# Pooling rows, gate additions and head 0's transposes around the seam between the gate stage and branch 1

## The chip, the cores and the metric

The kernel runs on one core of one Trainium2 chip. The metric is device time in microseconds (us) of one execution; three executions of the kernel before gave 874.96, 876.73 and 877.03 us, median 876.73 us. Lower is better.

## The reference

One encoder layer on 512 tokens of width 1024, all in float32:

```
proj = rms_norm(x) @ w_in           -> u_pool, u_lru, q, k, v, gate logits (3 x 1024)
gates = sigmoid(logits + b_gate)
pool:  for each of 4 groups of 256 channels (windows 2, 4, 8, 16):
         mean over the last w tokens, minus the token; then @ w_pool[g]; * pool_scale
lru:   width-4 convolution, two block-diagonal gates, a scan over the tokens
attn:  8 heads of 128, normalised q and k, strictly causal stick-breaking weights
merged = sum over branches of gates[b] * (y[b] @ w_branch[b])
x = x + merged @ w_out;  x = x + SwiGLU feed-forward(rms_norm(x))
```

## The kernel before

Every float32 product is taken as three matmuls of split operands (high times high, high times low, low times high). So nearly every operand is first split: ScalarE writes the high half (`act(..., AF.Copy)`), VectorE subtracts it from the source and writes the low half. For weights this is `split_w` (lines 142 and 143: `whi`, `wlo`); for pooled rows `split_hl` (L1040, L1041: `p00h`, `p00l` for group 0, half 0); for the pooling weights L1076 and L1077 (`wph`, `wpl`). Channels lie on the partitions, the 512 tokens along the free axis.

The kernel is written with a tile framework. The program lists the work; a planner at build time orders the instructions of each engine by their place in the program (a smaller place goes first, `tc.high_priority(n)` moves an instruction n places ahead) and by when a cost model says that they are ready, and assigns buffers. On the chip, each engine then runs its list in that fixed order and waits at semaphores. Two tools tie the order by hand: `tc.issue_after(ins)` puts what is traced inside it behind `ins` on `ins`'s engine, and `tc.add_manual_dep(a, b.name, ...)` does it for one pair. Neither adds a wait on the chip between engines.

The stages that matter here, in program order:

- **Pooling input** (249 to 287.7 us): 14 products `ps_ux`, `ps_uy` give u_pool in two chunks cc of 512 channels, each as two tiles j. The row (cc, j, n) is 128 channels; the group is 2 * cc + n. `pool_mean` (lines 945 to 961) makes a row's sliding-window mean on VectorE: for windows above 2 a short scan (L956), a long scan (L957), a short correction (L959) and the subtraction of the token (L961), with `pw` as the tile between. There are eight rows. Three run in this stage, the others in the next one.
- **Third branch's gates** (287.7 to 325.4 us): two chunks cc, each seven products `ps_gx`, `ps_gy` of 24 matmuls (L360). After product S4 of a chunk `gate_done` adds the bank `ps_gx` to the tile `gx` on VectorE (L939), after product 22 it does so for `ps_gy` and `gy`; ScalarE then takes two sigmoids (L941), and the POOL queue stores the tile (L943). In chunk 1, `pool_mean` is called after each of the products 12, S2, S1, S3 and S4 as long as rows are left; the last four rows, those of groups 2 and 3, run here. `load_early` fetches the weights of branch 1's first three half chunks, which are split here too.
- **Attention and the first two branches** (325.4 to some 474 us): `branch(1, c)`, c = 0 to 3, multiplies the scan's output `yHH`, `yHL` by `w_branch[1]`; a chunk is two half chunks of 24 matmuls (`half_chunk`; k-tiles 0 to 3, then 4 to 7; within a half, 12 matmuls for output tile j = 0 and 12 for j = 1), bank `ps_br` (L351 to L353); `merge` (L451) multiplies the result by its gate and frees the bank. `branch(0, c)` does the same with the pooled rows. Between them `tick()` pops attention tasks: a head's q and k are transposed (`trans`, L1131, tiles `pq`), split (L1134 `qkh`, L1135 `qkl`), multiplied into scores `z`, ScalarE takes sigmoids `K` and `A` (L1164, L1165), VectorE scans (`E`, L1168) and multiplies (`A`, L1170), the weights are transposed back (`pw`, L1181) and split (L1183, `wtl` L1184), and `py` is the head's output. `trans` of head 0 is first in program order in this stage. The pooled rows are split and multiplied by `w_pool` in `pool_split` and `pool_back` (banks `pps`, results `yph`, `ypl`), for all four groups ahead of branch 1 in program order.

[...] As the planner placed it, the last `ps_gx` lay on banks 0 and 1 and the last `ps_gy` on banks 4 and 5. In the next stage, head 0's `pq` of q is on bank 5, that of k on bank 7, the first `ps_br` on bank 0, the second on bank 2, and the third bank of that pool is 1. So head 0's first transposes can begin only when `gate_done` has read the last `ps_gy`, and branch 1's first matmuls when it has read the last `ps_gx`.

The scan's output comes back from DRAM in eight loads of 512 KB on the POOL queue (L1286: `yHH`, `yHL`); the last four of them, k-tiles 4 to 7, overwrite memory that the gate products read until S4 of chunk 1. SP's queue carries the other loads: `rawp` (w_pool, L1074), `raw` (branch weights, L150), `at` (q, k, v of a head, L1124), `g` (gates, L1101).

Of the kernel before, what the change touches and what calls it, by code (L numbers as in the profile page):

```python
# [12 lines left out]
ALU = mybir.AluOpType  # L13
# [3 lines left out]
P = 128  # L17
S = 512
D = 1024
KT = D // P  # L20
# [45 lines left out]
def layer_kernel(ctx: ExitStack, tc: tile.TileContext, x, xt, vecs, w_in, w_qkv7, w_gate7, w_pool7, w_pool, w_rg, w_ig,  # L66
# [282 lines left out]
    def mm3(ps, lh, ll, rh, rl, start, stop, skip=False, b=H):  # L349
        rh, rl = il(rh, b), il(rl, b)  # L350
        nc.tensor.matmul(ps, lh, rh, start=start, stop=False, skip_group_check=skip)  # L351
        nc.tensor.matmul(ps, lh, rl, start=False, stop=False, skip_group_check=skip)  # L352
        nc.tensor.matmul(ps, ll, rh, start=False, stop=stop, skip_group_check=skip)  # L353

# [54 lines left out]
    def half_chunk(pss, key, half, rhs, nticks, lo_last=False):  # L409
        wh, wl = weights(*key, half)  # L410
        if lo_last:

            for lo in range(2):
                for j in range(2):
                    for k in range(4 * half, 4 * half + 4):
                        for w, r in (((wl, 0),) if lo else ((wh, 0), (wh, 1))):
                            nc.tensor.matmul(pss[j], w[:, k % 4, j * P:(j + 1) * P], il(rhs[k][r]),
                                             start=k == 0 and not lo and r == 0,
                                             stop=k == KT - 1 and bool(lo))
            return  # L420
        for j in range(2):
            for kk in range(4):
                k = 4 * half + kk
                cs = slice(j * P, (j + 1) * P)
                mm3(pss[j], wh[:, kk, cs], wl[:, kk, cs], rhs[k][0], rhs[k][1],
                    k == 0, k == KT - 1)
            tick(nticks[j] if type(nticks) is tuple else nticks)
# [56 lines left out]
    with ExitStack() as first:  # L484
# [452 lines left out]
        def gate_done(cc, j, t, ps):  # L937
            v = two2(t)
            dve.tensor_tensor(v, v, in_order2(ps), ALU.add)  # L939
            for w in range(2):  # L940
# [4 lines left out]
        def pool_mean(cc, j, n):  # L945
# [43 lines left out]
        for cc in range(2):  # L989
# [11 lines left out]
            for nm in ORDER:  # L1001
# [42 lines left out]
    with ExitStack() as mix:  # L1044
# [27 lines left out]
        def load_pool_weights(g):  # L1072
            raw = rawp[g]
            state["rawp"] = nc.sync.dma_start(raw, w_pool[g].rearrange("(k p) c -> p k c", p=P)).ins  # L1074
            hi, lo = slot_r(f"wph{g}", (2, 256)), slot_r(f"wpl{g}", (2, 256))
            act(hi, raw, AF.Copy)  # L1076
# [34 lines left out]

        ysb = {}

        def head_tasks(h):
# [12 lines left out]
            def trans():  # L1127
                for t, gcol in ((0, qg), (1, vcol("k_norm"))):
                    pt = paux.tile([P, S], F32, tag="aux", name=f"pq{h}{t}")
                    for s in range(NS):  # L1130
                        nc.tensor.transpose(pt[:, s * P:(s + 1) * P], st["raw", t][:, s, :], idn)  # L1131
                    a = slot_r(f"qkh{h}{t}")
# [134 lines left out]
        tick(4)  # L1267
        for h in range(2):
            for g in (2 * h, 2 * h + 1):
                load_pool_weights(g)  # L1270
            if h:
                head0()
            for g in (2 * h, 2 * h + 1):
                for j in range(2):
                    pool_split(g, j)
        for g in range(4):
            for j in range(2):
                pool_back(g, j)
            tick()

# [10 lines left out]
        for c in range(4):  # L1291
            branch(1, c, ylru)
        hstack.close()

# [536 lines left out]
```

## Time and profile before

| | |
|---|---|
| median of 3 executions | 876.73 us (874.96 to 877.03) |
| profiled execution: its time, its span | 874.58 us, 872.8 us |
| granted TensorE clock, mean | 0.998 |
| TensorE (PE) busy | 859.7 us, 98% of the span |
| VectorE (DVE) busy | 748.5 us, 86% |
| ScalarE (ACT) busy | 528.3 us, 61% |
| GpSimd (POOL) busy | 96.6 us, 11% |
| DMA | 156.73 MB, mean 180 GB/s |

In the lists of instructions the columns are start in us, duration in us, engine, line, operation, output and inputs, and how often; a bracket at the end gives the idle time of the engine just ahead of it and what ended it ("issue": nothing that the profile shows). Where two operations of VectorE follow each other closely, the second starts a little ahead of the first's listed end, so steps are best taken from start to start. PEld is the weight load of a matmul, which overlaps with PE. "Granted clock" (PEclk) is the share of the full clock that TensorE had. A DMA's duration in these lists is that of its issue; when it lands is given apart.

### The profile page before, as it was taken

The page shows a single profiled execution, that of the slowest core. Times are in us where ns is not written, and L with a number is a line of the kernel's source. Part 1 is how long each engine was busy: PE and PEld are TensorE (multiplying, and loading weights), DVE is VectorE, ACT ScalarE, POOL GpSimd, SP SyncE. Part 2 cuts the span into 40 slices and gives each one's busy share as a digit, 9 for nine tenths or more (in the row PEclk, how much of TensorE's full clock was granted, in tenths as well). Part 3 has the DMA queues.
Part 4 walks back from the last instruction along what each step waited for, and adds up shares of the span by engine and source line. Part 5 has one row for each costly group of instructions (what it writes and reads, how often), then busy time and mean ns, then how long its engine had stood idle before and what let it go on. Part 6 is the DMA issues. An engine that isn't in the chain of part 4 may idle for free.

```text
span 872.8 us, 14573 instructions
## 1 busy us (share of the span) xinstructions
PE 859.7 (98%) x5707; PEld 791.0 (91%) x5707; DVE 748.5 (86%) x949; ACT 528.3 (61%) x733; POOL 96.6 (11%) x137
## 2 busy tenths in 40 slices
PE   9999999999999999999999999999999999999998
PEld 7888878888899997888889998889999999999998
DVE  6899897998786996997988696699998888899974
ACT  6554989657864466675664554455555555755642
POOL 1110002232325121000001200000000000031200
PEclk9999999999999999999999999999999999999999
DMA  9686356899598489545636865346543343798913
GB/s 340 165 294 191 97 168 193 239 296 260 194 269 232 93 240 303 184 129 153 210 97 168 177 186 193 97 121 169 140 127 98 104 115 107 230 247 201 195 36 122
DMA packets 114325, 156.73 MB, mean 180 GB/s; under 512 B 8272, under 2 KB 86096, under 8 KB 114256
## 3 DMA queue, kind: packets, MB, share of 16 engines
q1 hardware_dynamic: 100864, 107.30, 38.4%
q0 software_dynamic: 13248, 48.24, 23.9%
q8 instruction: 45, 0.74, 0.3%
q10 hardware_dynamic: 144, 0.26, 0.1%
q14 instruction: 24, 0.20, 0.1%
HBM read 135.33 MB, written 18.87 MB: 177 GB/s over the span
## 4 chain that ended last, share of the span: by engine, by line
PE 87%; DVE 5%; ACT 4%; issue 2%; DMA 1%; SPq 0%; DVEq 0%; ACTq 0%
PE ps_y L360 11%; PE ps_q L876 8%; PE ps_x L360 8%; PE ps_dy L1749 6%; PE ps_dx L1749 5%; PE ps_br L351 3%; PE ps_br L352 3%; PE ps_br L353 3%; PE ps_bY L1373 2%; PE ps_gy L360 2%; PE ps_gate L779 2%; PE ps_gx L360 2%; PE ps_uy L360 2%; PE ps_bX L1373 2%; PE ps_lru L351 1%
## 5 line engine op out<-in xcount | busy, mean ns | idle before, releaser
L142 ACT ACTIVATE whi<-raw 128x1024 fp32r<-128x1024 f32 x58 | 61.1, 1054 | 56.3 <-PE ps_out L352 15.1
L143 DVE TENSOR_TENSOR wlo<-raw,whi 128x1024 fp32r<-128x1024 f32 x58 | 70.9, 1223 | 12.3 <-ACT whi L142 11.4
L142 ACT ACTIVATE whi<-qw 128x1024 fp32r<-128x1024 f32 x48 | 50.4, 1054 | 30.2 <-PE ps_q L876 11.9
L143 DVE TENSOR_TENSOR wlo<-qw,whi 128x1024 fp32r<-128x1024 f32 x48 | 58.3, 1221 | 10.3 <-ACT whi L142 10.3
L1534 ACT ACTIVATE wh_S<-w_S 128x1024 fp32r<-128x1024 f32 x36 | 38.3, 1063 | 28.7 <-PE ps_y L360 20.0
L1655 POOL DMA_DIRECT2D dw<-in_w_down_dram x20 | 17.3, 882 | 303.7 <-DMA dw<-in_w_down_dram 260.6
L1535 DVE TENSOR_TENSOR wl_S<-w_S,wh_S 128x1024 fp32r<-128x1024 f32 x36 | 44.0, 1224 | 3.3 <-ACT wh_S L1534 3.3
L1534 ACT ACTIVATE wh<-w 128x1024 fp32r<-128x1024 f32 x27 | 28.7, 1064 | 27.7 <-PE ps_x L360 9.4
L1535 DVE TENSOR_TENSOR wl<-w,wh 128x1024 fp32r<-128x1024 f32 x27 | 33.1, 1225 | 7.9 <-ACT wh L1534 7.9
L1534 ACT ACTIVATE whdS<-dw 128x1024 fp32r<-128x1024 f32 x20 | 21.3, 1063 | 21.0 <-PE ps_dy L1749 10.6
L1168 DVE TENSOR_TENSOR_SCAN E<-K,ahead 128x512 f32<-128x512 f32 (+3 forms) x32 | 25.4, 816 | 8.7 <-ACT K L1164 8.7
L1535 DVE TENSOR_TENSOR wldS<-dw,whdS 128x1024 fp32r<-128x1024 f32 x20 | 24.3, 1223 | 5.5 <-ACT whdS L1534 5.5
L351 PE MATMUL ps_br<-yHH,whi 128*128 128x512 f32 x64 | 24.9, 390 | 0.1
L352 PE MATMUL ps_br<-yHL,whi 128*128 128x512 f32 x64 | 24.6, 384 | 0.0
L351 PE MATMUL ps_lru<-HH,whi 128*128 128x512 f32 x64 | 24.6, 384 | 0.0
L351 PE MATMUL ps_br<-yph,whi 128*128 128x512 f32 x64 | 24.5, 383 | 0.0
L353 PE MATMUL ps_br<-yHH,wlo 128*128 128x512 f32 x64 | 24.4, 384 | 0.0
L143 DVE TENSOR_TENSOR wlo<-pw,whi 128x1024 fp32r<-128x1024 f32 x13 | 15.8, 1223 | 10.0 <-ACT whi L142 8.6
L351 PE MATMUL ps_gate<-HH,whi 128*128 128x512 f32 x64 | 24.4, 381 | 0.0
L352 PE MATMUL ps_lru<-HL,whi 128*128 128x512 f32 x64 | 24.3, 379 | 0.0
L353 PE MATMUL ps_lru<-HH,wlo 128*128 128x512 f32 x64 | 24.3, 379 | 0.0
L352 PE MATMUL ps_gate<-HL,whi 128*128 128x512 f32 x64 | 24.3, 379 | 0.0
(786 smaller groups left out, 3552.2 us busy)
## 6 DMA issues: line engine op xcount, KB each, us to landing
qw<-in_w_qkv_dram SPq DMA_DIRECT2D x24, 512.0 KB, 7.0
raw<-in_w_in_dram SPq DMA_DIRECT2D x23, 512.0 KB, 5.6
dw<-in_w_down_dram POOLq DMA_DIRECT2D x20, 512.0 KB, 7.8
w<-in_w_ffn_gate_dram SPq DMA_DIRECT2D x36, 256.0 KB, 4.0
w<-in_w_ffn_up_dram SPq DMA_DIRECT2D x36, 256.0 KB, 4.6
raw<-in_w_branch_dram SPq DMA_DIRECT2D x13, 512.0 KB, 3.9
qw<-in_w_qkv_dram POOLq DMA_DIRECT2D x12, 512.0 KB, 7.7
qd<-r POOLq DMA_DIRECT2D x12, 512.0 KB, 6.8
```

Source lines behind the costliest of these rows:

```text
L142: act(hi, raw, AF.Copy)
L143: los.append(dve.tensor_tensor(lo, raw, hi.bitcast(F32), ALU.subtract).ins)
L351: nc.tensor.matmul(ps, lh, rh, start=start, stop=False, skip_group_check=skip)
L352: nc.tensor.matmul(ps, lh, rl, start=False, stop=False, skip_group_check=skip)
L353: nc.tensor.matmul(ps, ll, rh, start=False, stop=stop, skip_group_check=skip)
L360: nc.tensor.matmul(o, a_[a][:, w, k, :], il2(b_[b][:, k, :]), start=first and n == k == 0, stop=last and n == 2 and k == 3, skip_group_che ...
L876: nc.tensor.matmul(ps[:, a, :], b_[:, k, ts_], il(a_[:, kk, :]), start=first and n == k == 0, stop=n == 2 and k == 3, skip_group_check=True)
L1168: dve.tensor_tensor_scan(E[:, c0:c0 + n][:, ::-1], K[:, c0 + 1:c0 + n + 1][:, ::-1], ahead[:, S - n:][:, ::-1], 0.0, ALU.mult, ALU.add)
L1373: nc.tensor.matmul(o, ah[x_][:, w, k, :], il2(b[k][y_]), start=first_ and n == k == 0, stop=n == 2 and k == 3, skip_group_check=True)
L1534: act(h, src, AF.Copy)
L1535: dve.tensor_tensor(l, src, h.bitcast(F32), ALU.subtract)
L1749: nc.tensor.matmul(o, a_[a][:, w, k0 + k, :], il2(b_[b][:, k, :]), start=first and i == k == 0, stop=last and i == 2 and k == nk - 1, skip ...
```

## The change

Four edits go together.

1. In the gate stage `gate_done`'s addition gets 60 places of priority, and the one that comes last (chunk 1, j = 1, the `gy` tile) is remembered in `state["last"]`. The gate stage calls `pool_mean` once, after product S2 of chunk 0, and no more in chunk 1; the four rows that are left, all of them of groups 2 and 3, are called after the stage's last product and are tied behind `state["last"]` on VectorE.
2. `load_pool_weights` is cut in two: the loads of all four groups are called together, and `split_pool_weights` is called with each group.
3. Groups 0 and 1 are split and multiplied as before ahead of branch 1, with two ticks after each where there was one after each of four groups. Groups 2 and 3 are split and multiplied after `branch(1, 0)`, tied behind the last weight split that has been traced by then.
4. The eight transposes of head 0 are tied behind the last of the 24 matmuls of branch 1's first half chunk on TensorE.

The three matmuls in `mm3`, the number of pooling rows, splits, transposes and products, and what they compute, stay as they were.

```diff
@@ half_chunk
-                mm3(pss[j], ..., k == 0, k == KT - 1)
+                last = mm3(pss[j], ..., k == 0, k == KT - 1)
+            state.setdefault((key, half, j), last)
             tick(nticks[j] if type(nticks) is tuple else nticks)
@@ gate_done
-            dve.tensor_tensor(v, v, in_order2(ps), ALU.add)
+            with tc.high_priority(60):
+                last = dve.tensor_tensor(v, v, in_order2(ps), ALU.add).ins
+            if cc and j:
+                state["last"] = last
@@ pool_mean
-            with tc.issue_after(los[-1]):
+            with tc.issue_after(state["last"] if "last" in state else los[-1]):
@@ the gate stage's loop
-                if (cc or nm == "S2") and nm not in ("11", "22") and means:
+                if (cc, nm) == (0, "S2"):
                     pool_mean(*means.pop(0))
+        for row in means:
+            pool_mean(*row)
@@ the attention stage
-        for h in range(2):
-            for g in (2 * h, 2 * h + 1):
-                load_pool_weights(g)
-            if h:
-                head0()
-            for g in (2 * h, 2 * h + 1):
+        for g in range(4):
+            load_pool_weights(g)
+        head0()
+
+        def pool_group(g, edge):
+            with edge:
+                split_pool_weights(g)
                 for j in range(2):
                     pool_split(g, j)
-        for g in range(4):
+
+        for g in range(2):
+            pool_group(g, nullcontext())
+        for g in range(2):
             for j in range(2):
                 pool_back(g, j)
-            tick()
+            tick(2)
...
         for c in range(4):
             branch(1, c, ylru)
+            if c == 0:
+                for g in range(2, 4):
+                    pool_group(g, tc.issue_after(los[-1]))
+                    for j in range(2):
+                        pool_back(g, j)
+            if c == 0:
+                for tr in first_trans:
+                    tc.add_manual_dep(tr, state[("br", 1, 0), 0, 1].name, ...NoSync...)
```

More of the change, by code (lines that the diff above doesn't have):

```diff
@@ L352, in mm3 @@
         nc.tensor.matmul(ps, lh, rl, start=False, stop=False, skip_group_check=skip)
[L353 removed]
+        return nc.tensor.matmul(ps, ll, rh, start=False, stop=stop, skip_group_check=skip).ins
     def product(a_, b_, ps, half, first, last, ws=(0, 1)):
@@ L1074, in load_pool_weights, with split_pool_weights @@
             state["rawp"] = nc.sync.dma_start(raw, w_pool[g].rearrange("(k p) c -> p k c", p=P)).ins
+        def split_pool_weights(g):
+            raw = rawp[g]
             hi, lo = slot_r(f"wph{g}", (2, 256)), slot_r(f"wpl{g}", (2, 256))
@@ L1130, in trans @@
                     for s in range(NS):
-                        nc.tensor.transpose(pt[:, s * P:(s + 1) * P], st["raw", t][:, s, :], idn)
+                        tr = nc.tensor.transpose(pt[:, s * P:(s + 1) * P], st["raw", t][:, s, :], idn).ins
+                        if h == 0:
+                            first_trans.append(tr)
                     a = slot_r(f"qkh{h}{t}")
```

7 lines of the change are left out of this document (5 added, 2 removed).

## The prediction

> **What bounds the kernel now.** I read the page's busy shares, then the waits of TensorE, then the instructions around the longest one, then busy time by stretch.
>
> ```profile
> PE 859.7 (98%) x5707; PEld 791.0 (91%) x5707; DVE 748.5 (86%) x949; ACT 528.3 (61%) x733; POOL 96.6 (11%) x137
> ```
>
> TensorE is busy for 859.7 of 872.8 us, and the change takes no matmul away. All that it can win lies in the 13.1 us of idle time and in matmuls that run slowly. The waits of TensorE (us in total, times, longest) show one large one:
>
> ```profile
> PE pq L1131 <- issue: 3.7, 1, 3.7
> ```
>
> It is head 0's transposes, at the seam that the change edits. Here are TensorE's instructions there, and, from a warm stretch, the same eight transposes and three matmuls again:
>
> ```profile
> 325.12 0.28 PE L360 MATMUL ps_gy<-hT4h,wlo 128*128 128x256 f32 x1
> 329.11 1.94 PE L1131 MATMUL pq<-idn,at 128*128 128x128 f32 x8 [3.72 <-issue]
> 331.99 0.38 PE L351 MATMUL ps_br<-yHH,whi 128*128 128x512 f32 x1
> 332.21 0.38 PE L352 MATMUL ps_br<-yHL,whi 128*128 128x512 f32 x1
> ...
> 418.05 1.04 PE L1131 MATMUL pq<-idn,at 128*128 128x128 f32 x8
> 419.58 0.38 PE L351 MATMUL ps_br<-yph,whi 128*128 128x512 f32 x1
> ```
>
> What does it wait for? VectorE's list answers:
>
> ```profile
> 312.29 0.17 DVE L956 TENSOR_TENSOR_SCAN pw<-u,zero 128x8 f32<-128x8 f32 x1
> 314.46 1.22 DVE L143 TENSOR_TENSOR wlo<-qw,whi 128x1024 fp32r<-128x1024 f32 x1
> ...
> 322.22 0.18 DVE L956 TENSOR_TENSOR_SCAN pw<-u,zero 128x16 f32<-128x16 f32 x1
> 324.40 1.22 DVE L143 TENSOR_TENSOR wlo<-rawbr,whi 128x1024 fp32r<-128x1024 f32 x1
> 325.53 1.22 DVE L939 TENSOR_TENSOR gx<-gx,ps_gx 128x1024 f32<-128x1024 f32 x1
> 326.66 1.22 DVE L143 TENSOR_TENSOR wlo<-rawbr,whi 128x1024 fp32r<-128x1024 f32 x1
> 327.80 1.22 DVE L939 TENSOR_TENSOR gy<-gy,ps_gy 128x1024 f32<-128x1024 f32 x1
> 329.15 1.23 DVE L143 TENSOR_TENSOR wlo<-rawbr,whi 128x1024 fp32r<-128x1024 f32 x1
> 331.05 0.75 DVE L1135 SCALAR_TENSOR_TENSOR qkl<-pq,qg,qkh 128x512 fp32r<-128x512 f32 x1 [0.67 <-ACT qkh L1134]
> 340.92 1.22 DVE L1168 TENSOR_TENSOR_SCAN E<-K,ahead 128x512 f32<-128x512 f32 x1 [7.76 <-ACT K L1164]
> ```
>
> The `gy` addition ends at 329.02, and the transposes, whose bank it frees, start at 329.11. It is late because VectorE spent 312.29 to 324.40 on four pooling rows between weight splits. The `gx` addition began only at 325.53, though its product was over by 322.9, when a load that waits for the same product went out; and the split of branch 1's first weights ran at 324.40, though its high half had been begun at 319.95:
>
> ```profile
> 319.95 1.06 ACT L142 ACTIVATE whi<-rawbr 128x1024 fp32r<-128x1024 f32 x1 [1.13 <-PE ps_gy L360]
> 322.90 0.53 POOL L1286 DMA_DIRECT2D yHL<-ydl  x1 [10.30 <-PE ps_gx L360]
> ```
>
> The table by stretch (busy us of PE, PEld, DVE, ACT, POOL with their counts, then granted clock, DMA share, GB/s) shows what follows:
>
> ```profile
> 325.40:329.10 3.70, 0.00 (x0) 0.02 (x1) 3.61 (x4) 2.26 (x3) 0.54 (x1) 0.91 0.90 258
> 329.10:332.00 2.90, 2.89 (x12) 2.68 (x13) 2.17 (x3) 2.83 (x6) 1.26 (x4) 0.53 1.06 359
> 332.00:340.90 8.90, 8.90 (x45) 7.91 (x44) 1.16 (x2) 1.06 (x3) 1.32 (x4) 1.00 0.98 333
> 340.90:385.40 44.50, 43.12 (x225) 34.97 (x224) 42.08 (x64) 34.79 (x66) 0.00 (x0) 1.00 0.59 177
> 385.40:476.00 90.60, 90.04 (x508) 80.29 (x507) 80.22 (x141) 55.80 (x115) 3.51 (x4) 1.00 0.52 147
> ```
>
> Three things are to be seen. The stall leaves TensorE at 0.53 of its clock until 332. VectorE then has a hole, 332.0 to 340.9, with 1.16 us of work. And from 340.9 to 385.4 VectorE is busy for 42.08 of 44.5 us: there it is as much the limit as TensorE, and only after 385.4 does it have room again (80.22 of 90.6).
>
> **The change part by part.** *Stall.* With the rows out of the way, the `gx` addition runs at about 323 and ends before 325.4, so branch 1's first bank is free. Its first weights can be split at about 321. Branch 1's 24 matmuls then follow the last gate product directly, 24 x 0.215 = 5.2 us (step 331.99 to 332.21), to 330.6. The `gy` addition runs at 325.45 to 326.67 below them, so the transposes find their bank free. The 3.72 us go. If the cover fails (branch 1's operands late), the transposes would still start at 326.7, so 2.3 of the 3.72 stay won.
>
> *Clock.* From 329.11 to 331.99 eight transposes and three matmuls take 2.88 us; warm, from 418.05 to 419.58, the same take 1.53. The stall so costs another 1.35 us, and TensorE's gain is 3.72 + 1.35 = 5.07 us. [...]
>
> *Rows.* A row takes 2.17 us (312.29 to 314.46), and the last 2.18, so the four take 8.69 us. They are moved from a place where VectorE's time was, in part, free to right behind the `gy` addition. What VectorE gets: the addition ends 2.35 us earlier (326.67 for 329.02); the hole of 7.76 and the 0.67 us ahead of `qkl` can be filled. What it pays is 8.69. So VectorE as a whole gets ahead by 2.35 + 7.76 + 0.67 - 8.69 = 2.1 us, against TensorE's 5.1. The two weight splits and the `gx` addition of 324.40 to 327.80 move into the place that the rows leave.
>
> *What the difference does.* Low halves feed TensorE, and in 340.9 to 385.4 weight loads already wait for VectorE:
>
> ```profile
> PEld pq L1131 <- DVE wtl L1184: 1.1, 2, 0.8
> PEld z L352 <- DVE qkl L1135: 0.7, 2, 0.4
> ```
>
> A TensorE that comes 5.1 us early meets operands that come 2.1 us early, and waits more often. VectorE can win at most its idle 44.5 - 42.08 = 2.4 us more by 385.4, so the stage's gain has the bounds 2.1 and 4.5 us, and below 2.1 if the order leaves new holes on VectorE. I take 2.8, near the lower end: of these 2.4 us, 1.9 are three waits of `ypl` for `yph`
>
> ```profile
> DVE ypl L1095 <- ACT yph L1094: 1.9, 3, 0.7
> ```
>
> in the pooling groups, and I give a third of them, 0.7 us, to the groups' being spread out; nothing else in the change touches the rest.
>
> *Groups 2 and 3 later.* No work is added. Their rows are ready at about 337.6 (326.67 + 8.69, and two weight splits of 1.14 that go first). Before, their first split came 14 us after that:
>
> ```profile
> 351.81 0.69 DVE L1041 TENSOR_TENSOR p20l<-u,p20h 128x512 fp32r<-128x512 f32 x1
> ```
>
> So I cost this at nothing. The cover is branch 1's first chunk and groups 0 and 1; without it, groups 2 and 3 would wait for the rows, some 8.7 us at most.
>
> *Queues.* SP's loads of w_pool go into memory that no row of the four uses, and were out by 319.4, ahead of the seam; they cost nothing. But `raw` loads wait for the splits that free their buffer, and these come earlier. POOL's loads of the scan's output keep their place, behind the gate products:
>
> ```profile
> 300.28 19.11 SPq L1074 DMA_DIRECT2D rawp<-in_w_pool_dram  x4
> 324.45 0.57 POOL L1286 DMA_DIRECT2D yHL<-ydl  x1
> DMA to landing us min/median/max: 8.5/8.5/8.5
> 325.64 0.37 SPq L150 DMA_DIRECT2D raw<-in_w_branch_dram  x1
> 327.91 0.37 SPq L150 DMA_DIRECT2D raw<-in_w_branch_dram  x1
> ```
>
> (The line on landing is that of the `yHL` load of 324.45.) It lands at 333.0. The second half chunk starts at 330.6 + 0.8 (transposes) = 331.4 and reaches k-tile 6, which needs it, six matmuls later, at 332.7: a wait of 0.3 us, where before the half chunk came after the landing. TensorE is ahead of VectorE by then, so I add nothing.
>
> *Sum.* 5.1 us won on TensorE, 2.3 given back between 336 and 385 for VectorE's low halves: 2.8 us. The profiled execution took 874.58 us (span 872.8 and 1.8 around it) and would take 871.8. It was 2.15 us below the median of 876.73; on the median, I predict 873.9 us.
>
> **The rivals.** *TensorE keeps all of it.* If the planner fills the wait with branch matmuls (the third bank of `ps_br` takes 12 more, 2.6 us) and VectorE catches up in the roomier stretch after 385.4, all 5.1 us stay: 871.6 us. For it: TensorE waited little after 385.4 (90.04 of 90.6 busy). Against it: VectorE's 2.1.
>
> *A transfer takes the stall's place.* DMA is at 1.06 of its share from 329.1 to 332 and 0.98 to 340.9. Two `raw` loads of 512 KB come some 3 us earlier and share with the scan's output. Each is 1.4 us at 359 GB/s; if both go ahead, the last `yHL` lands at 335.8 and TensorE waits 3.1 us from 332.7. Of these 2.3 are what it would have waited for VectorE anyway, and 0.8 more are lost; where the later waits don't shrink for it, nearly all is. The time is 874.7 to 876.7, say 875.3.
>
> *Slower: the rows stand ahead of head 0 and the pooling splits.* VectorE runs its list in order, and the four rows are earlier in the program than `qkl` and `p00l`. The case has such a block already, on ScalarE:
>
> ```profile
> 283.76 0.69 DVE L961 SCALAR_TENSOR_TENSOR u<-pw,u 128x512 f32<-128x512 f32 x1
> 340.13 0.69 ACT L1164 ACTIVATE K<-z,qrs 128x512 f32<-128x512 f32 x1 [7.84 <-PE z L353]
> 341.81 0.63 ACT L1040 ACTIVATE p00h<-u 128x512 fp32r<-128x512 f32 x1
> ```
>
> Row 0 is ready at 284.4, yet its `p00h` stands behind `K`. With the rows first, until 337.6, two `qkl` (1.4 us) end at 339.0 and six splits of groups 0 and 1 (0.6 each) at 342.6. TensorE is through with branch 1's first chunk at 331.4 + 5.2 = 336.6. If its list has `pps` next, it waits until 342.6: 6.0 us, and 1.35 for the clock, which is 7.4 against 5.1 won: 2.3 us slower, 879.0 us. It decides from a wait of about 5 us; with `z` or 12 branch matmuls next the wait is 2.4 us or less, which is my forecast. [...]
>
> **How the numbers follow.** Chances: my forecast 0.48, all kept 0.20, transfer 0.15, slower 0.17. The forecast's own range is 872.2 (2.1 + 2.4 us) to 875.2 (1.5 us: the lower end with one new hole on VectorE of about the 0.67 us ahead of `qkl`). The whole range runs from 871.3, just past the full gain, to 878.0, halfway into the slower case. A measurement of this kernel tells about 0.3% from no change, 2.6 us, so faster begins below 874.1. All of the second case and two thirds of the first lie there: 0.52. The last third of the first and most of the transfer's give 0.29 within, and the slower case with a remainder 0.19.
>
> **What would show it.** Right: no wait of `pq` at 325; the first `ps_br` within 0.2 us of the last `ps_gy`; clock 1.00 from 325 to 332; the `gx` addition ending before 325.4; VectorE without the hole ahead of the first `E`, busy from 326.7 to about 342; more or longer waits of TensorE for `qkl`, `p..l` and `wtl` between 336 and 385, by some 2 us. Wrong: a wait of the first `ps_br` for the `gx` addition or a weight split; a wait for `yHL` beyond 1 us near 332; a single wait above 5 us at the first `pps` or `z`; or waits between 340 and 385 no larger than before, which would leave all 5.1 us.

## The result

The changed kernel took 872.3 us (median of 5 runs, 871.77 to 872.74) and the kernel before 876.73 us (median of 5 runs beside it, 873.88 to 877.28): a ratio of 0.9958, 95% interval 0.994 to 0.9976, so 2.1 to 5.3 us faster. Timed once more on another occasion it took 872.09 us against 874.32, a ratio of 0.9977 (0.9963 to 0.999). Both say faster; the first occasion's 4.4 us is not all the change's doing, as the stage lengths below show.

The profiled execution took 872.3 us with a span of 870.5 (before: 874.58 and 872.8).

### The profile page after: what moved, and what is told of

The parts are those of the page before. It is cut to its first block, busy times and chain, and to the rows that moved or that the text cites. A ratio compares the mean times of both kernels' runs of the same rounds, so it can differ in the third digit from the quotient of the medians.

```text
span 870.5 us, 14573 instructions
## 1 busy us (share of the span) xinstructions
PE 859.6 (99%) x5707; PEld 789.9 (91%) x5707; DVE 748.4 (86%) x949; ACT 528.2 (61%) x733; POOL 95.1 (11%) x137
## 4 chain that ended last, share of the span: by engine, by line
PE 86%; DVE 6%; ACT 5%; DMA 2%; issue 1%; SPq 0%; DVEq 0%; ACTq 0%
PE ps_y L360 11%; PE ps_q L877 8%; PE ps_x L360 8%; PE ps_dy L1774 6%; PE ps_dx L1774 5%; PE ps_uy L360 2%; PE ps_gate L780 2%; PE ps_bY L1398 2%; PE ps_gy L360 2%; PE ps_br L353 2%; PE ps_br L352 2%; PE ps_br L351 2%; PE ps_gx L360 2%; PE ps_bX L1398 2%; PE ps_ux L360 2%; PE ps_lru L351 1%
## 5 line engine op out<-in xcount | busy, mean ns | idle before, releaser
L1180 DVE TENSOR_TENSOR_SCAN E<-K,ahead 128x512 f32<-128x512 f32 (+3 forms) x32 | 25.4, 816 | 2.0 <-ACT K L1176 2.0
L353 PE MATMUL ps_gate<-HH,wlo 128*128 128x512 f32 x64 | 24.3, 379 | 0.0
```

The costliest lines, as they stand in the source:

```text
L353: return nc.tensor.matmul(ps, ll, rh, start=False, stop=stop, skip_group_check=skip).ins
L1180: dve.tensor_tensor_scan(E[:, c0:c0 + n][:, ::-1], K[:, c0 + 1:c0 + n + 1][:, ::-1], ahead[:, S - n:][:, ::-1], 0.0, ALU.mult, ALU.add)
```

## The profile after

The lines of code have moved: `gate_done`'s addition is L941, the pooling rows are L960 to L965, the transposes L1141, `qkl` L1147, `E` L1180, the loads of the scan's output L1302. The busy shares, from the page, are as good as the same; it is the span that is shorter.

```profile
PE 859.6 (99%) x5707; PEld 789.9 (91%) x5707; DVE 748.4 (86%) x949; ACT 528.2 (61%) x733; POOL 95.1 (11%) x137
```

TensorE's instructions at the seam, from the timeline:

```profile
325.18 0.28 PE L360 MATMUL ps_gy<-hT4h,wlo 128*128 128x256 f32 x1
325.30 0.38 PE L351 MATMUL ps_br<-yHH,whi 128*128 128x512 f32 x1
330.48 1.04 PE L1141 MATMUL pq<-idn,at 128*128 128x128 f32 x8
332.72 0.48 PE L351 MATMUL ps_br<-yHH,whi 128*128 128x512 f32 x1
334.26 0.48 PE L352 MATMUL ps_br<-yHL,whi 128*128 128x512 f32 x1 [1.05 <-DMA yHL<-ydl]
335.55 0.38 PE L353 MATMUL ps_br<-yHH,wlo 128*128 128x512 f32 x1
337.09 0.48 PE L352 MATMUL z<-qkl,qkh 128*128 128x512 f32 x1 [1.16 <-DVE qkl L1147]
```

The 3.72 us stall is gone: branch 1 follows the last gate product after 0.12 us, and the transposes take 1.04 us where they took 1.94. Two waits that weren't there stand behind them: 1.05 us for the last load of the scan's output, and 1.16 us for head 0's low half. The profile counts idle time from the modelled end of the matmul before; from start to start each wait is longer. From 332.72 to 334.26 it is 1.54 us, and from 335.55 to 337.09 as well, where such matmuls otherwise start 0.22 us apart; the matmul behind each starts 0.10 us late too (334.58 and 337.41). So TensorE loses 1.4 us at each. VectorE's timeline shows what that low half was behind:

```profile
322.82 1.22 DVE L941 TENSOR_TENSOR gx<-gx,ps_gx 128x1024 f32<-128x1024 f32 x1 [0.47 <-PE ps_gx L360]
...
325.50 1.22 DVE L941 TENSOR_TENSOR gy<-gy,ps_gy 128x1024 f32<-128x1024 f32 x1 [0.32 <-PE ps_gy L360]
326.63 1.22 DVE L143 TENSOR_TENSOR wlo<-rawbr,whi 128x1024 fp32r<-128x1024 f32 x1
327.77 0.33 DVE L960 TENSOR_TENSOR_SCAN pw<-u,zero 128x8 f32<-128x8 f32 x3
...
335.02 0.69 DVE L965 SCALAR_TENSOR_TENSOR u<-pw,u 128x512 f32<-128x512 f32 x1
335.63 0.74 DVE L1147 SCALAR_TENSOR_TENSOR qkl<-pq,qg,qkh 128x512 fp32r<-128x512 f32 x1
336.29 0.74 DVE L1147 SCALAR_TENSOR_TENSOR qkl<-pq,vt,qkh 128x512 fp32r<-128x512 f32 x1
...
338.68 1.23 DVE L1180 TENSOR_TENSOR_SCAN E<-K,ahead 128x512 f32<-128x512 f32 x1 [1.04 <-ACT K L1176]
```

The four rows run from 327.77 to 335.63 (7.86 us, their parts woven into one another), then `qkl`, on which `z` waits. Head 0's high halves had been written by 332.38 (`qkh` on ScalarE), so it is the rows that hold `qkl` back. The profile lists no idle time of VectorE from 325.50 to the end of the second `qkl` at 337.03, and `z` starts 0.06 us after that. The table by stretch (busy us of PE, PEld, DVE, ACT, POOL with their counts, then granted clock, DMA share, GB/s):

```profile
325.20:330.50 5.30, 5.30 (x28) 4.61 (x27) 5.00 (x9) 2.63 (x4) 2.60 (x7) 1.00 1.13 316
330.50:332.00 1.50, 1.50 (x12) 1.42 (x11) 1.50 (x3) 0.88 (x2) 0.74 (x2) 1.00 1.12 381
332.00:340.90 8.90, 6.37 (x29) 4.42 (x28) 7.82 (x14) 3.92 (x9) 0.00 (x0) 1.00 1.05 354
340.90:385.40 44.50, 43.34 (x232) 35.56 (x231) 41.92 (x64) 33.65 (x63) 0.00 (x0) 1.00 0.60 174
385.40:473.80 88.40, 87.83 (x494) 78.31 (x493) 78.26 (x138) 54.68 (x114) 3.51 (x4) 1.00 0.52 145
```

The clock stays at 1.00. TensorE's new idle time, 2.53 us, lies in the third stretch. In the fourth, where the prediction expected it, TensorE idles 44.50 - 43.34 = 1.16 us; before it was 44.50 - 43.12 = 1.38.

**A cleaner measure than the median.** The executions of the kernel before scatter over some 4 us, so I take the length of the stage that the change edits: from the start of the last `ps_gy` matmul to that of the first `ps_bY`, the first product after the attention stage. Its end rows in the kernel before and in the changed one:

```profile
474.26 0.27 PE L1373 MATMUL ps_bY<-B11h,whi 128*128 128x256 f32 x1
```

```profile
472.07 0.27 PE L1398 MATMUL ps_bY<-B11h,whi 128*128 128x256 f32 x1
```

With 325.12 and 325.18 as their starts: 149.14 us before, 146.89 after. Two other stretches of the same profiles, worked out in the same way, are not the change's: from the first `ps_u` to the last `ps_gy`, and from the first `ps_y` to the last matmul. The fourth column is the first part of the seam stage: from the start of the last `ps_gy` to that of the first `z` matmul that reads a `qkl`. In every kernel of the table 46 other matmuls lie between them (8 transposes, 36 of branch 1, 2 of `z`). All profiles of this study but one (the filled stall further down, which has ten matmuls more and another order behind):

| kernel | first `ps_u` to last `ps_gy` | **seam stage** | of it up to the first `z<-qkl` | first `ps_y` to last matmul |
|---|---|---|---|---|
| before | 76.14 | **149.14** | 14.32 | 273.01 |
| before, again | 74.93 | **149.16** | 14.34 | 276.83 |
| changed | 75.71 | **146.89** | 11.91 | 273.03 |
| changed, again | 75.57 | **146.96** | 11.99 | 273.79 |
| changed, timed again | 74.92 | **146.95** | 12.00 | 273.02 |
| without edit 4 | 74.92 | **146.96** | 12.00 | 274.84 |
| without edit 3 | 74.93 | **146.84** | 12.00 | 273.01 |
| without edit 1 | 76.15 | **145.68** | 10.83 | 273.02 |
| edit 4 alone | 74.92 | **145.58** | 10.76 | 275.32 |
| three rows back | 75.68 | **144.99** | 10.14 | 275.29 |
| three rows back, again | 74.93 | **145.01** | 10.14 | 273.01 |
| three rows back, small loads | 75.54 | **145.75** | 10.88 | 273.00 |

The seam stage of one kernel repeats within 0.07 us, in the three kernels that were profiled more than once; the outer columns move by 1.2 and by 3.8 us, also between two profiles of the same kernel. So the change won 2.25 us (149.14 to 146.89), and differences of 1 us between variants can be read from this column where the medians can't carry them. The fourth column says where they arise: what is left of the stage behind that `z` is 134.82 to 134.98 us in every kernel. So nearly all that these edits win or lose lies in the first 10 to 14 us.

## The experiments

The theory behind the first runs was the prediction's: the edits together take the stall away, and VectorE's lateness takes part of it back. Each of the first four undoes one part of the change.

**Without edit 4.** The changed kernel, with the transposes free to go where the planner puts them:

```diff
             if c == 0:
-                for tr in first_trans:
-                    tc.add_manual_dep(tr, state[("br", 1, 0), 0, 1].name, ...NoSync...)
```

> The change without its fourth edit: head 0's transposes are not tied behind branch 1's first 24 matmuls, and come first on TensorE again. The theory (a late addition held the transposes' bank; two waits then give part of it back) expects: the gy addition ends at about 326.7 as in the changed kernel, so the transposes wait some 1.3 us from 325.4, too short to cost much clock; the second half chunk comes 1.3 us later and so no longer waits for the load of the scan's output (1.05 us in the changed kernel). Together within 0.5 us of the changed kernel, 872 to 873 us. The rival (the tie is what removes the stall) expects a wait of 3 us or more for the transposes and 875 us or more.

871.67 us, ratio 0.9973 (0.9961 to 0.9984). TensorE's timeline:

```profile
325.65 1.06 PE L1141 MATMUL pq<-idn,at 128*128 128x128 f32 x8 [1.36 <-issue]
333.62 0.48 PE L352 MATMUL ps_br<-yHL,whi 128*128 128x512 f32 x1 [0.22 <-DMA yHL<-ydl]
336.01 0.48 PE L352 MATMUL z<-qkl,qkh 128*128 128x512 f32 x1 [0.71 <-DVE qkl L1147]
```

The transposes now wait 1.36 us, and the clock stays at 1.00 from 324 to 332. But the waits behind them shrink by as much (1.05 to 0.22, 1.16 to 0.71): those operands come when they come, and a TensorE that is 1.4 us later finds them nearer. The seam stage is 146.96 against 146.89: given the other edits, edit 4 is worth nothing. With or without it, `z` starts 11.9 to 12.0 us after the last `ps_gy`, when the second `qkl` is there.

**Without edit 1.** The rows back between the weight splits of the gate stage, no priority for the additions; edits 2 to 4 kept:

```diff
-            with tc.high_priority(60):
-                last = dve.tensor_tensor(v, v, in_order2(ps), ALU.add).ins
-            if cc and j:
-                state["last"] = last
+            dve.tensor_tensor(v, v, in_order2(ps), ALU.add)
...
-            with tc.issue_after(state["last"] if "last" in state else los[-1]):
+            with tc.issue_after(los[-1]):
...
-                if (cc, nm) == (0, "S2"):
+                if (cc or nm == "S2") and nm not in ("11", "22") and means:
                     pool_mean(*means.pop(0))
-        for row in means:
-            pool_mean(*row)
```

> The change without its first edit: the four pooling rows and the gate additions stand in the gate stage as before, everything else is as in the changed kernel, and TensorE's list is the same. The theory expects the first bank of branch 1 to wait for the gx addition until about 326.8, 1.4 us, and in return no wait of z for qkl (1.16 us in the changed kernel) and none for the load of the scan's output (1.05 us), as VectorE has 8.7 us less to do behind the seam: 870.5 to 872.5 us, no slower than the changed kernel. The rival (moving the rows is what wins) expects the stall of 3 us or more back at the first matmul of branch 1, and 875 us or more.

870.61 us, ratio 0.9959 (0.9946 to 0.9973); seam stage 145.68. TensorE, and then VectorE:

```profile
326.70 0.48 PE L351 MATMUL ps_br<-yHH,whi 128*128 128x512 f32 x1 [1.48 <-DVE gx L940]
```

```profile
325.43 1.21 DVE L940 TENSOR_TENSOR gx<-gx,ps_gx 128x1024 f32<-128x1024 f32 x1
333.34 0.75 DVE L1142 SCALAR_TENSOR_TENSOR qkl<-pq,qg,qkh 128x512 fp32r<-128x512 f32 x1 [3.06 <-ACT qkh L1141]
337.25 1.23 DVE L1175 TENSOR_TENSOR_SCAN E<-K,ahead 128x512 f32<-128x512 f32 x1 [1.91 <-ACT K L1171]
```

One wait of 1.48 us for the `gx` addition, and then neither `yHL` nor `qkl` is waited for beyond 0.3 us. VectorE has holes of 3.06 and 1.91 us again, and yet the stage is 1.2 us shorter than with edit 1. Edit 1 as a whole, in a kernel that has edit 4, costs 1.2 us net.

**Three rows back.** One row alone stays behind the `gy` addition; the priority stays:

```diff
-                if (cc, nm) == (0, "S2"):
+                if (cc, nm) == (0, "S2") or cc and nm in ("12", "S2", "S1"):
                     pool_mean(*means.pop(0))
```

> The changed kernel with three of its four moved rows back in the gate stage (after its products 12, S2 and S1) and only the last one behind the gy addition; TensorE's list is the same. The theory expects both gate additions on time (no wait at 325), the wait of z for qkl gone, the load's wait of 1.05 us still there, and fewer waits of TensorE for VectorE up to 385: 1.2 to 2.5 us below the changed kernel, 869.8 to 871.1 us. The rival (VectorE's list behind the seam is no limit, the waits at qkl only move TensorE's idle time) expects 872.0 to 872.6 us, as the changed kernel.

871.56 us, ratio 0.9963 (0.9948 to 0.9977); seam stage 144.99, the shortest. TensorE's timeline:

```profile
329.89 1.04 PE L1141 MATMUL pq<-idn,at 128*128 128x128 f32 x8
333.23 0.48 PE L352 MATMUL ps_br<-yHL,whi 128*128 128x512 f32 x1 [0.79 <-DMA yHL<-ydl]
```

No wait at the seam, none over 0.3 us for `qkl`, and 0.79 us for the load. Against the kernel without edit 1 the stage is 0.7 us shorter, with the additions on time; so the priority and one moved row together cost nothing, and what costs 1.9 us in the changed kernel is that three more rows stand ahead of `qkl`. The total missed what was expected: the last stage took 275.29 us in the profile, 2.3 more than in most others, in code that is the same. A later run settles that.

**Without edit 3.** All four pooling groups ahead of branch 1, as in the kernel before, the other edits kept:

```diff
-        for g in range(2):
+        for g in range(4):
             pool_group(g, nullcontext())
-        for g in range(2):
+        for g in range(4):
             for j in range(2):
                 pool_back(g, j)
-            tick(2)
+            tick()
...
-            if c == 0:
-                for g in range(2, 4):
-                    pool_group(g, tc.issue_after(los[-1]))
-                    for j in range(2):
-                        pool_back(g, j)
```

> The changed kernel with its third edit undone: pooling groups 2 and 3 are split and multiplied ahead of branch 1 in program order again, with one tick after each group. The theory gives the spreading 0.7 us of the forecast's 2.8 (a third of the 1.9 us of waits for yph): 872.7 to 873.5 us, with waits of ypl for yph of about 1.9 us. The rival (the cover is needed: groups 2 and 3 would wait for the late rows) expects a wait of TensorE for p20l or p30l above 2 us and 874.5 us or more.

871.48 us, ratio 0.9968 (0.9956 to 0.998); seam stage 146.84 against 146.89. VectorE's waits (us in total, times, longest) from 325 to 390, in this variant:

```profile
DVE ypl L1104 <- ACT yph L1103: 1.8, 3, 0.7
```

and in the changed kernel:

```profile
DVE vl L1154 <- ACT vh L1153: 1.3, 1, 1.3
DVE qkl L1147 <- ACT qkh L1146: 0.9, 1, 0.9
```

The spreading does take the three waits of `ypl` away, and about as much of other waits on VectorE takes their place. TensorE waits elsewhere than in the changed kernel:

```profile
330.85 0.46 PE L351 MATMUL ps_br<-yHH,whi 128*128 128x512 f32 x1 [0.68 <-DMA yHH<-ydh]
334.06 0.48 PE L352 MATMUL ps_br<-yHL,whi 128*128 128x512 f32 x1 [1.18 <-DMA yHL<-ydl]
```

It stands longer for the loads, 1.86 us in all, and then only 0.10 us for `qkl`. Yet `z` starts 12.00 us after the last `ps_gy`, as in the changed kernel. While four rows stand ahead of `qkl`, the waits for the loads are hidden in the one that ends with `qkl`. Behind `z` the stage takes 134.84 us in this variant and 134.98 in the changed kernel, so the spreading wins nothing there either.

**Edit 4 alone.** If edit 1 costs 1.2 us beside edit 4, and edit 3 nothing, then the tie alone in the kernel before should do as well as without edit 1 (the lines that remember the last matmul, as in the change, are left out here):

```diff
@@ the kernel before
                     for s in range(NS):
-                        nc.tensor.transpose(pt[:, s * P:(s + 1) * P], st["raw", t][:, s, :], idn)
+                        tr = nc.tensor.transpose(pt[:, s * P:(s + 1) * P], st["raw", t][:, s, :], idn).ins
+                        if h == 0:
+                            first_trans.append(tr)
...
             branch(1, c, ylru)
+            if c == 0:
+                for tr in first_trans:
+                    tc.add_manual_dep(tr, state[("br", 1, 0), 0, 1].name, ...NoSync...)
```

> The kernel before with edit 4 alone: head 0's eight transposes behind the first 24 matmuls of branch 1; the four pooling rows, the order of the groups and the loads stay as in the kernel before. Theory (edit 4 alone takes the stall away, and moving the rows costs a little over 1 us): the same matmul order as in the variant with the rows in their old place, so a wait of some 1.4 us for the addition of gx or gy stays in front of the first ps_br, no long wait for the transposed inputs at 325, none over 0.5 us for yHL or qkl; the stretch from the last ps_gy to the first ps_bY about 145.7 us, against 149.1 in the kernel before and 146.9 in the changed one; the total some 3 us under the kernel before. Rival (edit 4 needs edits 1 and 3: with the old order of the groups, VectorE and the transfers are late for the transposes wherever they stand): the stretch stays at 148 us or more, with a wait of 2 us or more at the transposes or at the first ps_br, and the total within 1 us of the kernel before.

871.78 us, ratio 0.9953 (0.9935 to 0.9972). TensorE's timeline:

```profile
323.67 0.28 PE L360 MATMUL ps_gy<-hT4h,wlo 128*128 128x256 f32 x1
325.35 0.48 PE L351 MATMUL ps_br<-yHH,whi 128*128 128x512 f32 x1 [1.40 <-DVE gx L940]
330.63 1.04 PE L1133 MATMUL pq<-idn,at 128*128 128x128 f32 x8
...
469.25 0.27 PE L1381 MATMUL ps_bY<-B11h,whi 128*128 128x256 f32 x1
```

145.58 us: 3.56 us under the kernel before, by one edit. The two ways to end the stall don't add up. Edit 4 alone wins 3.56; edits 1 to 3 without it win 2.18; all four win 2.25. The fourth column shows why: with edit 1 the four rows keep `z` from starting before 11.9 us, whatever TensorE waits for until then, and without edit 1 it starts at 10.8. The stage of this variant was profiled once, and the intervals of its ratio and of the changed kernel's overlap; the comparison rests on the stage.

**Three rows back, the last loads in halves.** What is left there is the wait for `yHL`. The four loads of 512 KB become eight of 256 KB, in the order of use, on top of the edit above:

```diff
-            for k2 in range(2):
+            step = 1 if i else 2
+            for k in range(0, 4, step):
                 for t, d in zip(yhl, yd):
-                    load = nc.gpsimd.dma_start(t[:, 2 * k2:2 * k2 + 2, :], d[i][:, 2 * k2:2 * k2 + 2, :]).ins
+                    load = nc.gpsimd.dma_start(t[:, k:k + step, :], d[i][:, k:k + step, :]).ins
```

> The variant with three rows back in the gate stage, and the last four loads of y (512 KB each) cut into eight of 256 KB in the order of use, so that the first slice that TensorE needs can land sooner. Theory (the wait for yHL is for the landing of these loads, whose bytes share the queue): the wait for yHL, 0.79 us in the variant with three rows back and 1.05 us in the changed kernel, falls under 0.3 us, and the stretch from the last ps_gy to the first ps_bY goes from 144.99 to 144.2 to 144.7 us; the total 869 to 871 us. Rival (the loads share the transfer engines and are all in flight together, so smaller ones land no sooner; four more issues on POOL also delay the stores of gx and gy by some 2 us): the wait for yHL stays at 0.6 to 1.2 us, the stretch at 145 us or more.

870.98 us, ratio 0.9941 (0.9921 to 0.9962). TensorE's timeline:

```profile
332.79 0.48 PE L352 MATMUL ps_br<-yHL,whi 128*128 128x512 f32 x1 [0.46 <-DMA yHL<-ydl]
333.71 0.48 PE L351 MATMUL ps_br<-yHH,whi 128*128 128x512 f32 x1 [0.22 <-DMA yHH<-ydh]
```

The one wait has become several: these two, 0.68 us together, and a short one of 0.13 us for `yHL` at 334.64. The first slice comes 0.14 us sooner (its wait ends 8.49 us after the last `ps_gy`, against 8.63 with large loads), and the next two come 0.9 and 1.9 us behind it. The first wait, 0.46 us, lies between what the theory and the rival expected; the seam stage, 145.75, is the rival's. It is 0.75 us longer than with large loads, and the fourth column has 0.74 of that (10.88 against 10.14): the waits for the loads, from start to start, are the whole difference. The median of 870.98 is no sign of the best variant, as the kernel before took 875.7 us beside it.

**The kernel before, again, and the changed kernel, again.** No edit; these are the measure of the measure.

> The kernel before, unchanged, for a second profile. Theory (the stretch from the last ps_gy to the first ps_bY is a property of the kernel, and the stages around it vary from run to run): the stretch 148.6 to 149.6 us again, the wait for the transposed inputs 3.4 to 4.0 us, and the clock lowered after it again. Rival (the lowered clock came by chance): the wait is the same and the clock stays at 1.00, and the stretch is some 1.3 us shorter, about 147.8 us.

> The changed kernel, unchanged, for a second profile. Theory: the stretch from the last ps_gy to the first ps_bY 146.6 to 147.2 us again, with one wait of about 1.1 us for yHL and one for qkl. Rival (these waits vary from run to run by as much as they are long): the stretch off by 0.7 us or more, in which case the differences of about 1.2 us between the variants are not shown.

877.72 us (one run) and 872.95 us (one run); seam stages 149.16 and 146.96. The stall is 3.73 us and the clock is lowered again in the second profile of the kernel before; the waits of the changed kernel are 1.05 and 1.21 us. Both theories held, so the differences in the table are the kernels'.

**Is the lowered clock from standing still?** Ten matmuls of 128x512 on a constant tile, in front of the first transposes of the kernel before, to keep TensorE at work during the stall:

```diff
@@ the kernel before
                     pt = paux.tile([P, S], F32, tag="aux", name=f"pq{h}{t}")
+                    if h == 0 and t == 0:
+                        for _ in range(10):
+                            nc.tensor.matmul(pt, warm, warm.unsqueeze(1).to_broadcast([P, 4, P]), start=True, stop=True)
                     for s in range(NS):
```

> The kernel before, with ten matmuls of 128x512 on a constant tile put on TensorE in front of head 0's first transposes; they write the tile that the transposes then overwrite, so nothing of the result changes. They start when that tile is free, about 1.5 us after the last ps_gy, and take about 2.2 us, so they fill most of the 3.7 us in which TensorE stood. Theory (the lowered clock after the stall is from standing still): the first transpose starts at the same distance from the last ps_gy, 4.0 us, but the granted clock stays at 1.00, and from the first transpose to the 25th ps_br of branch 1 it takes 6.0 to 6.2 us, as in the variant without edit 4 (6.08), against 7.42 in the kernel before. Rival (the lowered clock belongs to the load of that stretch, with DVE, ACT and all transfer engines busy): the clock is below 0.8 in the 2 us behind the first transpose also here, and the stretch takes 7.2 us or more. Work behind 336 us is in another order here, so neither the total nor the stretch up to the first ps_bY is compared.

875.73 us (one run). The filling failed, as TensorE's timeline shows:

```profile
324.04 0.28 PE L360 MATMUL ps_gy<-hT4h,wlo 128*128 128x256 f32 x1
327.99 4.43 PE L1132 MATMUL pq<-warm 128*128 128x512 bf16 x10 [3.67 <-DVE gy L939]
332.21 1.50 PE L1134 MATMUL pq<-idn,at 128*128 128x128 f32 x8
```

The fillers write the transposes' bank, and that bank comes free with the `gy` addition, not 1.5 us after the last product as I had thought. So they stood in the same stall and came on top of it. That settles one step of the prediction, which had only put together that the 3.72 us "issue" wait ended with that addition: here the profile names it. For the clock it gives something else. Granted clock by half microsecond (fourth number from the end is POOL's count, then clock, DMA share, GB/s), first the kernel before, again, then this variant:

```profile
327.50:328.00 0.50, 0.00 (x0) 0.00 (x0) 0.50 (x1) 0.50 (x2) 0.12 (x1) 0.87 0.95 270
328.00:328.50 0.50, 0.00 (x0) 0.00 (x1) 0.43 (x1) 0.50 (x1) 0.42 (x1) 0.50 1.11 393
331.00:331.50 0.50, 0.50 (x3) 0.38 (x3) 0.49 (x2) 0.50 (x2) 0.50 (x3) 0.72 1.04 361
331.50:332.00 0.50, 0.50 (x4) 0.45 (x3) 0.50 (x2) 0.21 (x1) 0.50 (x3) 1.00 1.12 391
```

```profile
326.00:326.50 0.50, 0.00 (x0) 0.00 (x0) 0.50 (x1) 0.50 (x2) 0.00 (x0) 0.81 0.99 229
331.00:331.50 0.50, 0.50 (x3) 0.22 (x2) 0.00 (x0) 0.00 (x0) 0.50 (x3) 0.50 1.06 371
333.00:333.50 0.50, 0.50 (x7) 0.50 (x5) 0.00 (x0) 0.20 (x1) 0.00 (x0) 0.86 1.08 363
```

In the second profile of the kernel before, the clock is at half from 327.87 to 331.28 (0.13 us of the first row's half, 0.28 of the third's, taking a row's mean as a step between the 0.50 and the 1.00 of the rows beside it): 3.41 us. In the variant it is at half from 326.31 to 333.14: 6.83 us, twice that, although DVE and ACT do nothing from 329.72 to the end of it (0.00 at 331.00). And without edit 4 the clock stays at 1.00 from 324 to 332, with DVE busy for 7.68 of the 8.00 us, a DMA share of 1.09 and a wait of 1.36 us; with edit 4 alone, after 1.40 us, likewise (1.00 from 324 to 332, at a DMA share of 1.03). So busy neighbours and transfers did not by themselves lower it here. What tells these profiles apart is how long TensorE stood: 3.73 us in the kernel before and 3.67 in the variant, against 1.36 and 1.40. The test as it was meant, the stall filled and nothing else changed, was not made.

**The best variant beside the changed kernel.** Both unchanged from above, on the same chip:

> The changed kernel, unchanged, timed on the same chip as the variant with three rows back in the gate stage. Theory: 871.5 to 872.8 us, 3 to 4.5 us under the kernel before there; stretch from the last ps_gy to the first ps_bY 146.8 to 147.0 us.

> The variant with three rows back in the gate stage once more, beside the changed kernel on the same chip. Theory (its shorter stretch is kept to the end): the stretch from the last ps_gy to the first ps_bY 144.9 to 145.1 us again, and the median 1.2 to 2.4 us under the changed kernel's. Rival (what the stretch gains is given back in the later stages, as the first profile with its 2.3 us longer last stage might be read): the stretch is as short, and the median is within 0.8 us of the changed kernel's.

872.09 us, ratio 0.9977 (0.9963 to 0.999), and 870.72 us, ratio 0.9953 (0.9941 to 0.9966). The start and the end of the seam stage with three rows back:

```profile
325.91 0.28 PE L360 MATMUL ps_gy<-hT4h,wlo 128*128 128x256 f32 x1
334.54 0.48 PE L352 MATMUL ps_br<-yHL,whi 128*128 128x512 f32 x1 [0.79 <-DMA yHL<-ydl]
...
470.92 0.27 PE L1398 MATMUL ps_bY<-B11h,whi 128*128 128x256 f32 x1
```

145.01 us again, and the last stage is 273.01 this time: the gain is not given back there, and the long last stage of the first profile was that execution's. The median is 1.4 us below the changed kernel's, the seam stage 1.9. The intervals of the two ratios still touch, so it is the stage, twice measured, that says this variant beats both kernels.

## Why the prediction was right, and where it wasn't

The forecast was 873.9 us with a range of 871.3 to 878.0, and faster as the likeliest; 872.3 is inside. In the stage that is edited, the forecast of 2.8 us compares with 2.25.

*Stall and clock: right.* The transposes don't wait, the first `ps_br` comes 0.12 us after the last `ps_gy`, the clock stays at 1.00. The 1.35 us for the clock is borne out: from the first transpose to the fourth `ps_br` the kernel before takes 2.88 us (329.11 to 331.99) and the variant without edit 4, which stands 1.36 us first, 1.55 (325.65 to 327.20). The 1.35 is less than half of the low stretch of 3.41 us, because TensorE stood through part of it: in the second profile of the kernel before the transposes start at 328.53, 0.66 us after it began, and half of 3.41 - 0.66 is 1.37.

*Rows: order right, size nearly.* The additions moved up as forecast (`gx` at 322.82, `gy` at 325.50), the rows stand behind them, and VectorE's 7.76 us hole is one of 1.04. They take 7.86 us and not 8.69.

*What the difference does: the failed step.* "A TensorE that comes 5.1 us early meets operands that come 2.1 us early, and waits more often", in 340.9 to 385.4. TensorE idles there 1.16 us, less than before, and from the first `z<-qkl` to the end of the stage it takes 134.98 us, where the kernel before took 134.82. VectorE was 42.08 of 44.5 us busy there and still did not set the pace. What was given back stands before 338, at one place: `z` can't start before the two `qkl` behind the four rows. From start to start the stall was 3.88 us (329.11 - 325.12 - 0.11); with 1.35 for the clock 5.2 us were won, and of these 2.25 stayed. The two waits, at 1.4 us each, are 2.8 of the 3.0 given back, and the 0.16 us behind `z` is the rest. Both come from `qkl`: as said under `yHL` below, a load on time would have made the second wait longer by the first. The forecast of 2.3 was near in size by luck, and wrong in place and cause: a queue order at one place, not the load of a stage. The proof is three rows back: with one row ahead of `qkl` instead of four that wait falls to 0.3 us or less, and the stage by 1.9. The prediction also took the rows' move for the means to end the stall and did not price the tie alone, which won 3.56.

*Spreading of the groups: 0.7 us credited, 0 measured* (146.84 without edit 3). The `ypl` waits do go, but they were VectorE's and not the path's; the same mistake from the other side.

*`yHL`: 0.3 us forecast and not added, 1.05 measured.* TensorE came in time (332.72 against the 332.7 forecast for k-tile 6) and the load later than 333.0. The answer of the trace for the loads issued last in the changed kernel:

```profile
DMA to landing us min/median/max: 8.7/9.2/9.7
```

against 8.5 before. Issued at 324.5, 9.7 us later is 334.2, when the wait ends. The rival that a transfer takes the stall's place was right in kind (DMA share 1.13 from 325.2), with 1.05 us for its 3.1. The reason given for adding nothing, that TensorE is ahead of VectorE by then anyway, holds, though for `qkl` alone and not for a whole stage. In the five profiles with four rows ahead of `qkl`, the waits listed for these loads are between 0.22 us (without edit 4) and 1.86 (without edit 3), and `z` starts at 11.91 to 12.00 us in all of them. The load costs time only once the rows are gone, as in three rows back.

*The slower rival* had the mechanism (the rows do stand ahead of `qkl`) and a price of 6.0 us; the wait was 1.16, since `z` was next on TensorE with 12 branch matmuls ahead, as the rival's own condition said.

*The number itself* came out below the forecast by luck: of the 4.4 us between the medians, 2.25 belong to the seam stage, and the profiled executions differ by as little (874.58 less 872.3); on the second occasion the medians differ by 2.2 us (874.32 less 872.09), as much as the stage.

## What to carry to other kernels

When several edits remove the same stall, price each alone: here reordering one engine's list (the tie of eight transposes) won 3.56 us, and adding to it the edit that moves the late work on the other engine out of the way took 1.2 us back. Before work is moved behind a seam, ask which short operation it will then stand in front of: with one pooling row there `qkl` was not waited for, with four the stage was 1.9 us longer. Before a wait is priced, ask which later wait it is hidden in: here four rows on VectorE made every wait of TensorE ahead of `z` free. An engine that is 95% busy in a stretch (here VectorE, 42.08 of 44.5 us) isn't its limit unless another engine waits for it there.

## What the runs showed of the hardware that I had not expected

The low stretches at the seam have a common length: 328.44 to 331.85 in the first profile of the kernel before (the half microseconds from 328.00 and 331.50 show 0.94 and 0.65, those between them 0.50) and 327.87 to 331.28 in the second are 3.41 us each, and the 6.83 us with the fillers are twice that. Why, no run here shows. The ten fillers ran from 327.99 and took 4.43 us, and the clock stayed at half to 333.14 all the same: TensorE was at work for the last 5.15 us of that stretch. Waits of 1.36, 1.40 and 1.48 us left the clock at 1.00 (without edit 4, edit 4 alone, without edit 1). Two shorter ones, close together, were once followed by half the clock, in the last stage of the second profile of the kernel before, from 798.91 to 802.32 (the mean clock of that execution is 0.996, against 0.998 in the first profile):

```profile
796.00 1.06 ACT L1534 ACTIVATE whd<-dr 128x1024 fp32r<-128x1024 f32 x1 [6.78 <-DMA dr<-in_w_down_dram]
797.11 0.38 PE L1749 MATMUL ps_dx<-Bd120h,whd 128*128 128x256 f32 x1 [0.88 <-ACT whd L1534]
798.37 0.38 PE L1749 MATMUL ps_dx<-Bd120h,wld 128*128 128x256 f32 x1 [0.77 <-DVE wld L1535]
```

In the first profile of three rows back the same two waits, 0.72 and 0.77 us, left the clock at 1.00. Nearly the same waits were followed by half the clock in one execution and by the full clock in the other; what decides between them, no run here shows.

These rows also say why the stretch from the first `ps_y` to the last matmul, the same code in every kernel here, took from 273.00 to 276.83 us: a load of down-projection weights (`dr`) comes late, ScalarE's split waits for it, and TensorE for the split. ScalarE waits 6.78 us for it at 276.83, 6.62 and 6.64 at 275.29 and 275.32, and 4.00 at 273.01 in the second profile of three rows back, where TensorE doesn't wait there. The lowered clock adds, by my estimate, some 1.7 us in the longest, half of 3.41. Why the load is late in some executions stays open. The stage before the seam took 74.92 to 76.15 us, for which no reason is shown here. All this is more than the change is worth, and only the seam stage's own length, which repeats within 0.07 us, made the variants comparable.
